# A decoder block on one core: operand tiles and row loads at the start of the feed-forward stage

## The chip, the core and the metric

The kernel runs on one core of one Trainium2 chip. A core has TensorE (PE; matmuls, with the load of the stationary operand shown as PEld), VectorE (DVE), ScalarE (ACT), GpSimd (POOL), SyncE (SP) and 16 DMA engines. All loads and stores of this kernel are issued from SP, in one queue, in a fixed order. The metric is the device time of one execution in microseconds. Three runs of the kernel before gave 2730.93 (median), 2728.78 and 2732.68 us.

## What is computed

One decoder layer for one sequence of 2048 tokens, model width 1024, all in float32. The first half is the token mixer (windowed attention beside an mLSTM, merged and projected); the second half, where the change lies, is a gated feed-forward stage of width 2816:

```python
mix = merged @ w_out[l]
x = x + gate_m[:, None, :] * rms_norm(mix, g_post_mix[l])
h2 = modulate(rms_norm(x, g_pre_ffn[l]), shift_f, scale_f)
ff = (jax.nn.silu(h2 @ w_ffn_gate[l]) * (h2 @ w_ffn_up[l])) @ w_ffn_down[l]
x = x + gate_f[:, None, :] * rms_norm(ff, g_post_ffn[l])
```

## The kernel before

**Precision.** A float32 product is made of three fast ones: each operand is split into a high part (a cast on ACT, line 1353) and a low part (source minus high part, on DVE, line 1354), and `mm` (line 204) issues high x high, high x low and low x high. A tile of 128 x 512 is a unit (256 KB), a tile of 128 x 2048 a big buffer (1 MB).

**Products of sums.** Each block product of 2 x 2 blocks is done with seven products instead of eight. `PROD` lists them as pairs of a weight block or weight sum (11, 12, S2, 22, S1, S3, S4) and an operand (11, 21, T2, T4, T1, T3, 22). The operands 11, 21, 22 are quarters of h2; T1 to T4 are sums of quarters. Every operand has a high and a low tile of four units each, seven pairs in all, kept in `HC` while the gate and up products run. T3 is read by the sixth product, 22 by the seventh.

**Building the operands.** `h_combine(b2, ...)` does that for one half (1024 tokens) of the sequence: for each of four steps k it loads the normalised rows `x1n`, transposes them on PE, scales and shifts them on ACT, forms the sums on DVE and splits them. For the first half it runs inside the last output projection of the mixer. There SBUF is short: three tiles (T2 high, T2 low, T4 high) lie in a pool `hcp` which takes the place of the closed mixer pool `kvp` (line 1362), and the others in big buffers, of which there are 14 (`big`). Two operands are parked: 22 goes to `hc_d` in DRAM (line 1416), and so does T3, of which only the high part is made (line 1418). `rest_of_hc` brings them back in the first gate/up pair: eight loads into units (line 1431), for 22 four casts (line 1433), and eight subtractions (line 1434).

**Gate and up.** `gate_up(b2)` runs 11 pairs p. A pair is seven gate parts, then seven up parts, of 12 matmuls each. Their results go through `combine` (P1 copied on ACT in line 1497, U2 in line 1503, U4 in line 1508) into 16 units in the pool `fpool`, which takes the place of the mixer's `mpool` and `tpool` (names `tm` and `tx`) once these are closed. For the first half each pair also loads two rows of down weights into a big buffer (line 1530), forms their sums and stores four (line 1539); sums of the previous pair's results are stored in line 1581, and results in line 1569.

**Late rows.** The last block's rows of x1 are normalised late: the pairs p = 1 to 4 of the first half end with `norm_rows(3, t)`, which loads a row tile in two halves (line 1548), squares them on ACT with a running sum (line 1549), forms the reciprocal root (POOL, line 475), scales on ACT (line 560) and stores to `x1n` (line 561), which the second half's `h_combine` reads.

**What sets the order.** The program is written as a stream of parts and steps; `run2` loads and prepares weights some parts ahead (four in gate and up). What is written is then ordered for each engine by a planner that plays the program against modelled durations and, whenever an engine is free, takes the earliest written instruction that is ready by its model. That order is fixed before the run; on the chip each engine waits for real. `tc.keep_in_program_order` pins an instruction behind everything written earlier on its engine. Buffers of one kind (units, big buffers) are handed out in written order as they come free.

Of the kernel before, what the change touches and what calls it, by code (L numbers as in the profile page):

```python
# [10 lines left out]
F32 = mybir.dt.float32  # L11
F32R = mybir.dt.float32r
I32 = mybir.dt.int32
U32 = mybir.dt.uint32
AF = mybir.ActivationFunctionType
ALU = mybir.AluOpType
# [3 lines left out]
P = 128  # L20
# [3 lines left out]
TB = 512  # L24
NT = TB // P
NBLK = S // TB
# [45 lines left out]
def decoder_block(ctx: ExitStack, tc: tile.TileContext, a: dict, out: bass.AP, dbg=None):  # L72
    nc = tc.nc
    V, A, G, T = nc.vector, nc.scalar, nc.gpsimd, nc.tensor
# [18 lines left out]
    def nm(s):  # L93
        uid[0] += 1
        return f"{s}{uid[0]}"
# [10 lines left out]
    def tm(shape, dtype=F32):  # L106
        return mpool.tile(shape, dtype, tag="tm", name=nm("tm"), bufs=9)

    def big(shape, dtype=F32):
        t = bpool.tile([P, 2048], dtype, tag="big", name=nm("big"))  # L110
        return t.rearrange("p (k c) -> p k c", k=shape[0])
# [64 lines left out]
    for i in range(HD // 2):  # L176
        f = np.float32(10000.0) ** np.float32(np.float32(-2.0) * np.float32(i) / np.float32(HD))
# [300 lines left out]
    HC, HR = {}, {}  # L478

    def hc_part(name, i):  # L480
        st = HC.setdefault(name, [None, None])
        if st[i] is None:
            st[i] = big([4, TB], F32R)
        return st[i]
# [135 lines left out]
    x1 = [tc.dram_tile([TB, D], F32, name=f"x1_{b}") for b in range(NBLK)]  # L620
# [719 lines left out]
    def unit():  # L1340
        if "pool" not in F:
            return tm([P, TB])
        return F["pool"].tile([P, TB], F32, tag="w", name=nm("w"), bufs=16)

    def quad(t):
        return t.rearrange("p (k c) -> p k c", k=4)

    def split_unit(src, hi=None, lo=None):
        if hi is None:
            t = split_tile("hl")  # L1350
            hi, lo = t[:, :TB], t[:, TB:]
        v = (lambda t: quad(t)) if len(src.shape) == 3 else (lambda t: t)
        A.copy(v(hi), src)  # L1353
        V.tensor_tensor(v(lo), src, v(hi).bitcast(F32), op=ALU.subtract)  # L1354
        return hi, lo
# [3 lines left out]
    def open_hc():  # L1359

        p1k.close()
        hcp = ctx.enter_context(tc.tile_pool(name="hcp", bufs=1, side="right", reuse_waits="tile"))
        HC.clear()
        t2h, t2l, t4h = [hcp.tile([P, 4, TB], F32R, name=f"hc{x}") for x in ("T2h", "T2l", "T4h")]
        hcp.tile([P, 8], F32, name="hc_end")
        HC["T2"] = [t2h, t2l]
        HC["T4"] = [t4h, None]

    def four(t):
        return [t[:, i * 4:(i + 1) * 4, :] for i in range(4)]  # L1370
# [4 lines left out]
    def h_combine(b2, rows, quarters, sums):  # L1375


        wait = b2 == 0
        QUADS = ((0, 0), (0, 1), (1, 0), (1, 1))

        def load(k):
            xk = rows()
            for j, (half, i) in enumerate(QUADS):
                c0 = (k + 4 * half) * P
                nc.sync.dma_start(xk[j], x1n[b2 * 2 + i][:, c0:c0 + P].rearrange("(t p) c -> p t c", p=P))
            return xk

        xn = load(0)
        yield 9000.0 if wait else 13000.0
        for k in range(4):  # L1390
            xk = xn
            v = {}
            for j, (half, i) in enumerate(QUADS):
                kk = k + 4 * half
                ps = mix_tile()
                for t in range(4):
                    transpose(ps[:, t * P:(t + 1) * P], xk[j][:, t, :])
                q = quarters()
                A.activation(q, ps, AF.Identity, scale=s2[:, kk:kk + 1], bias=sh2[:, kk:kk + 1])
                v[f"{half + 1}{i + 1}"] = q  # L1400
                if i:
                    yield 1500.0
            if k < 3:
                xn = load(k + 1)
            v["T1"] = sums()
            V.tensor_tensor(v["T1"], v["12"], v["11"], op=ALU.subtract)
            v["T2"] = sums()
            V.tensor_tensor(v["T2"], v["22"], v["T1"], op=ALU.subtract)
            V.tensor_tensor(v["12"], v["22"], v["12"], op=ALU.subtract)
            v["T3"] = v.pop("12")  # L1410
            for name in NAMES:
                if name == "T4":
                    v["T4"] = sums()
                    V.tensor_tensor(v["T4"], v["21"], v["T2"], op=ALU.subtract)
                if wait and name in ("T3", "22"):
                    nc.sync.dma_start(hc_d[:, ("T3", "22").index(name), k, :], v[name])
                    if name == "T3":
                        A.copy(hc_part("T3", 0)[:, k, :], v[name])
                else:
                    split_unit(v[name], hc_part(name, 0)[:, k, :], hc_part(name, 1)[:, k, :])  # L1420
                    if not wait:
                        yield 1500.0
            yield 10000.0 if wait else 1000.0

    hc_d = tc.dram_tile([P, 2, 4, TB], F32, name="hc_d")

    def rest_of_hc(i):
        name = ("T3", "22")[i]
        for k in range(4):
            u = unit()  # L1430
            nc.sync.dma_start(u, hc_d[:, i, k, :])
            if name == "22":
                tc.keep_in_program_order(A.copy(hc_part("22", 0)[:, k, :], u))
            tc.keep_in_program_order(V.tensor_tensor(hc_part(name, 1)[:, k, :], u, HC[name][0][:, k, :].bitcast(F32), op=ALU.subtract))  # L1434

    def a_operands(raw, spare):

# [101 lines left out]
                nc.sync.dma_start(ws_d[:, i, p, :], q[n])  # L1539
        return load, sums  # L1540

    def norm_rows(blk, t):
        sx = small.tile([P, 2], F32, tag="sx", name=nm("sx"), bufs=4)
        xy = []
        for h2 in range(2):
            c = slice(h2 * TB, (h2 + 1) * TB)
            xr, y0 = unit(), unit()
            nc.sync.dma_start(xr, x1[blk][t * P:(t + 1) * P, c])
            tc.keep_in_program_order(A.activation(y0, xr, AF.Square, accum_out=sx[:, h2:h2 + 1]))
            xy.append((xr, y0, c))  # L1550
        norm_out(xy, t, x1n[blk], sx)

    def gate_up(b2):
        late = None
        for p in range(NP):
            g = {}

            def done_g(qd, t, in_psum, g=g):
                g[qd] = unit()
                A.activation(g[qd], t, AF.Sigmoid)  # L1560
                V.tensor_tensor(g[qd], t, g[qd], op=ALU.mult)

            def done_u(qd, t, in_psum, p=p, g=g):
                V.tensor_tensor(g[qd], t, g[qd], op=ALU.mult)

                names = {"11": "11", "12": "21", "21": "12", "22": "22"}
                F["a", names[qd]] = g[qd]
                if qd != "12":
                    nc.sync.dma_start(as_d[b2][:, IDX[names[qd]], p, :], g[qd])
                    return  # L1570
                g["all"] = {n: F.pop(("a", n)) for n in ("11", "12", "21", "22")}

            def a_sums(p=p, g=g):
                a_ = g["all"]
                s1_, s2_, s4_ = unit(), unit(), unit()
                V.tensor_tensor(s1_, a_["21"], a_["22"], op=ALU.add)
                V.tensor_tensor(a_["21"], a_["11"], a_["21"], op=ALU.subtract)
                V.tensor_tensor(s2_, s1_, a_["11"], op=ALU.subtract)
                V.tensor_tensor(s4_, a_["12"], s2_, op=ALU.subtract)
                for n, t_ in (("S1", s1_), ("S3", a_["21"]), ("S2", s2_), ("S4", s4_)):  # L1580
                    nc.sync.dma_start(as_d[b2][:, IDX[n], p, :], t_)

            gp, up = (list(pair_parts(w, p * 256, done, unit, unit, mix_tile)) for w, done in ((wg, done_g), (wu, done_u)))
            load, sums = down_weights(p)
            if F.get("late") is not None and p == 0:
                def a_step():
                    if F["late"]:
                        F["late"].pop(0)()

                for part in gp + up:  # L1590
                    part.after = a_step
            yield from gp[:2]
            if b2 + p == 0:
                yield lambda: rest_of_hc(0)
            if late:
                yield late
            yield from gp[2:4]
            if b2 + p == 0:
                yield lambda: rest_of_hc(1)
            if b2 == 0:  # L1600
                yield load
            yield from gp[4:] + up[:3]
            if b2 == 0:
                yield sums
            yield from up[3:]
            late = a_sums
            if b2 == 0 and 1 <= p <= NT:
                yield lambda t=p - 1: norm_rows(NBLK - 1, t)
        yield late

    IDX = {x: i for i, (x, _) in enumerate(PROD)}
# [248 lines left out]
```

## Time and profile before

| | |
|---|---|
| runs shown | 2730.93 us median, 2728.78 to 2732.68 |
| profiled execution | 2731.52 us, of which the span from first to last instruction is 2729.8 us |
| granted TensorE clock, mean | 0.994 |
| last matmul of the mixer's output projection | 1417.90 us |
| gate and up, first half | from 1418.13 us |

A row of waits names the engine, tile and line that waited, then what it waited for, then the us in total, the number of times and the longest; the name of a line such as L204 is that of the helper which issued the instruction. In the order of time a row gives start, length, engine, line, operation, out<-in by the program's names, the count of merged instructions, and in brackets the idle time before and what ended it. A row of windows gives for a stretch its length, the busy time of PE, PEld, DVE, ACT and POOL (with counts), the granted PE clock, the DMA engines' busy share and GB/s.

### The profile page before, as it was taken

To read this page: it belongs to the slowest core of one execution; us is meant where nothing else is said; L and a number is where in the kernel's file an instruction comes from. 1 tells how busy PE (TensorE), PEld (TensorE's weight loads), DVE (VectorE), ACT (ScalarE), POOL (GpSimd) and SP (SyncE) were. 2 spreads that over 40 slices of the span, in tenths; PEclk is the share of its full clock that TensorE was granted. 3 is DMA by queue.
4 is the path that set the end of the run, shared out by engine and by line. 5 is a ranking of instruction groups with operands and counts; after the bars stand their busy time and mean duration, and the time that the engine had idled before them with its cause. 6 is when DMAs were issued, how large, how long until landed. Compare 5 with 4: busy or idle time off the path is not lost.

```text
span 2729.8 us, 35753 instructions
## 1 busy us (share of the span) xinstructions
PE 2641.6 (97%) x12310; PEld 2133.7 (78%) x12310; DVE 1999.4 (73%) x3954; ACT 1287.9 (47%) x2510; POOL 153.2 (6%) x189
## 2 busy tenths in 40 slices
PE   6998999999999899999999999999999999999998
PEld 4766688888877668888877878888777888888886
DVE  7959878767786978876677677776677666766456
ACT  5555644445755654344563443335554333333444
POOL 2010002100101000110000000000000000000000
PEclk8999999999999999999999999999999999999999
DMA  7754445687675545577765555446675332324566
GB/s 248 243 172 159 139 143 178 217 329 254 218 247 163 174 151 170 182 237 281 249 212 200 182 182 164 147 144 212 201 266 195 110 108 93 108 97 147 181 213 216
DMA packets 355222, 513.99 MB, mean 188 GB/s; under 512 B 25296, under 2 KB 213836, under 8 KB 349920
## 3 DMA queue, kind: packets, MB, share of 16 engines
q1 hardware_dynamic: 355040, 511.71, 56.5%
q8 instruction: 97, 1.59, 0.2%
q14 instruction: 85, 0.70, 0.1%
HBM read 358.17 MB, written 145.06 MB: 184 GB/s over the span
## 4 chain that ended last, share of the span: by engine, by line
PE 75%; DVE 8%; DMA 4%; issue 4%; ACT 2%; POOL 0%; SPq 0%; DVEq 0%; POOLq 0%; ACTq 0%
PE acc L204 53%; PE mix L204 21%; DVE hl L1354 2%; PE mix L209 1%; DMA w<-x 1%; ACT hl L1353 1%; DMA raw<-as_d 1%; DMA at_d<-tx 1%; DVE tx L1132 1%; DMA raw<-in_w_ffn_down_dram 0%; DMA tx<-in_w_ada_dram 0%; DVE tx L578 0%; DVE big L1354 0%; DMA w<-hc_d 0%; POOL rs L475 0%
## 5 line engine op out<-in xcount | busy, mean ns | idle before, releaser
L204 PE MATMUL acc<-big,hl 128*128 128x512 f32 x3936 | 946.6, 394 | 13.1 <-ACT tx L805 6.8
L204 PEld LDWEIGHTS acc<-big,hl 128*128 128x128 f32 x3936 | 733.8, 189 | 181.2 <-issue 10.1
L1353 ACT CAST hl<-raw 128x512 fp32r<-128x512 f32 x732 | 439.9, 621 | 488.8 <-PE acc L204 227.7
L1354 DVE TENSOR_TENSOR hl<-raw,hl 128x512 fp32r<-128x512 f32 x732 | 497.7, 696 | 193.0 <-ACT hl L1353 192.3
L204 PE MATMUL acc<-whi,big 128*128 128x512 f32 (+1 forms) x1280 | 378.8, 376 | 18.8 <-ACT big L518 8.4
L204 PE MATMUL mix<-big,hl 128*128 128x512 f32 x1232 | 333.9, 393 | 6.8 <-DVE big L1434 6.0
L204 PEld LDWEIGHTS acc<-whi,big 128*128 128x128 f32 x1280 | 234.3, 190 | 65.4 <-ACT big L518 8.5
L204 PEld LDWEIGHTS mix<-big,hl 128*128 128x128 f32 x1232 | 231.8, 188 | 58.5 <-DVE big L1434 6.4
L204 PE MATMUL acc<-wlo,big 128*128 128x512 f32 (+1 forms) x640 | 240.1, 378 | 4.1 <-DVE wlo L260 4.1
L204 PE MATMUL acc<-hl,hl 128*128 128x512 f32 x1008 | 237.1, 393 | 5.4 <-DVE hl L1354 3.5
L204 PEld LDWEIGHTS acc<-hl,hl 128*128 128x128 f32 x1008 | 186.9, 188 | 50.7 <-DVE hl L1354 9.1
L204 PE MATMUL mix<-hl,hl 128*128 128x512 f32 x792 | 183.0, 391 | 2.0 <-ACT hl L1353 1.0
L204 PEld LDWEIGHTS mix<-hl,hl 128*128 128x128 f32 x792 | 147.8, 188 | 36.3 <-DVE hl L1354 3.4
L260 DVE TENSOR_TENSOR wlo<-raw,whi 128x1024 fp32r<-128x1024 f32 (+1 forms) x96 | 109.3, 1138 | 73.0 <-ACT whi L259 66.6
L204 PE MATMUL acc<-big,whi 128*128 128x512 f32 x512 | 154.9, 391 | 0.0
L259 ACT CAST whi<-raw 128x1024 fp32r<-128x1024 f32 (+1 forms) x96 | 94.4, 984 | 126.2 <-PE acc L204 124.2
L204 PEld LDWEIGHTS acc<-wlo,big 128*128 128x128 f32 x640 | 121.9, 191 | 30.1 <-DVE wlo L260 5.6
L475 POOL TENSOR_TENSOR rs<-ms,nhalf 128x1 f32<-128x1 f32 (+1 forms) x56 | 43.1, 781 | 1652.0 <-DVE ms L473 1519.3
L204 PE MATMUL acc<-hcT2h,hl 128*128 128x512 f32 x352 | 118.4, 397 | 4.4 <-ACT w L1497 4.4
L204 PE MATMUL mix<-hcT4h,hl 128*128 128x512 f32 x352 | 117.4, 395 | 0.0
L204 PEld LDWEIGHTS acc<-big,whi 128*128 128x128 f32 x512 | 95.7, 188 | 19.5
L204 PE MATMUL acc<-big,wlo 128*128 128x512 f32 x256 | 96.4, 393 | 0.0
(332 smaller groups left out, 3392.7 us busy)
## 6 DMA issues: line engine op xcount, KB each, us to landing
raw<-in_w_in_dram SPq DMA_DIRECT2D x48, 1024.0 KB
as_d<-w SPq DMA_DIRECT2D x154, 256.0 KB
raw<-as_d SPq DMA_DIRECT2D x70, 512.0 KB
raw<-in_w_ffn_gate_dram SPq DMA_DIRECT2D x22, 1024.0 KB
raw<-in_w_ffn_up_dram SPq DMA_DIRECT2D x22, 1024.0 KB
raw<-ws_d SPq DMA_DIRECT2D x40, 512.0 KB
tx<-in_w_ada_dram SPq DMA_DIRECT2D x64, 256.0 KB
y_d<-tm SPq DMA_DIRECT2D x64, 256.0 KB
```

The lines of the kernel that those rows point to most:

```text
L204: T.matmul(o, lhsT=lhsT, rhs=rhs, start=start, stop=stop, skip_group_check=resumed)
L209: T.transpose(o, i, ident[:k, :k])
L259: A.copy(hv, src)
L260: V.tensor_tensor(lv, src, hv.bitcast(F32), op=ALU.subtract)
L475: G.tensor_tensor(r[:, :n], ms[:, :n], nhalf[:, :n], op=ALU.pow)
L1132: V.scalar_tensor_tensor(ac, u[:, j:j + TB], col("conv_w", j * 8 + f), ac, op0=ALU.mult, op1=ALU.add)
L1353: A.copy(v(hi), src)
L1354: V.tensor_tensor(v(lo), src, v(hi).bitcast(F32), op=ALU.subtract)
```

## The change

T4's low part gets a tile of its own in `hcp`. T3 is split fully inside `h_combine` (a subtraction instead of a store). Only 22 is parked; `load_22` brings it back by one load of 1 MB into the place of its own low part, and `split_22` casts and subtracts from there, both in the first pair, no longer pinned to the written order. `norm_rows` is divided: `load_late` issues the two loads between the gate parts and the up parts, `norm_late` does the rest at the end of the pair, its Squares no longer pinned.

```diff
-        t2h, t2l, t4h = [hcp.tile([P, 4, TB], F32R, name=f"hc{x}") for x in ("T2h", "T2l", "T4h")]
+        t2h, t2l, t4h, t4l = [hcp.tile([P, 4, TB], F32R, name=f"hc{x}") for x in ("T2h", "T2l", "T4h", "T4l")]
         hcp.tile([P, 8], F32, name="hc_end")
         HC["T2"] = [t2h, t2l]
-        HC["T4"] = [t4h, None]
+        HC["T4"] = [t4h, t4l]
...
-                if wait and name in ("T3", "22"):
-                    nc.sync.dma_start(hc_d[:, ("T3", "22").index(name), k, :], v[name])
-                    if name == "T3":
-                        A.copy(hc_part("T3", 0)[:, k, :], v[name])
+                if wait and name == "22":
+                    nc.sync.dma_start(hc_d[:, k, :], v[name])
                 else:
                     split_unit(v[name], hc_part(name, 0)[:, k, :], hc_part(name, 1)[:, k, :])
...
-    hc_d = tc.dram_tile([P, 2, 4, TB], F32, name="hc_d")
-
-    def rest_of_hc(i):
-        name = ("T3", "22")[i]
+    hc_d = tc.dram_tile([P, 4, TB], F32, name="hc_d")
+
+    def load_22():
+        nc.sync.dma_start(hc_part("22", 1).bitcast(F32), hc_d)
+
+    def split_22():
+        hi, lo = (hc_part("22", i) for i in range(2))
         for k in range(4):
-            u = unit()
-            nc.sync.dma_start(u, hc_d[:, i, k, :])
-            if name == "22":
-                tc.keep_in_program_order(A.copy(hc_part("22", 0)[:, k, :], u))
-            tc.keep_in_program_order(V.tensor_tensor(hc_part(name, 1)[:, k, :], u, HC[name][0][:, k, :].bitcast(F32), op=ALU.subtract))
+            split_unit(lo[:, k, :].bitcast(F32), hi[:, k, :], lo[:, k, :])
...
-    def norm_rows(blk, t):
+    rows = {}
+
+    def load_late(blk, t):
+        rows[t] = []
+        for h2 in range(2):
+            c = slice(h2 * TB, (h2 + 1) * TB)
+            rows[t].append((unit(), c))
+            nc.sync.dma_start(rows[t][-1][0], x1[blk][t * P:(t + 1) * P, c])
+
+    def norm_late(blk, t):
         sx = small.tile([P, 2], F32, tag="sx", name=nm("sx"), bufs=4)
         xy = []
-        for h2 in range(2):
-            c = slice(h2 * TB, (h2 + 1) * TB)
-            xr, y0 = unit(), unit()
-            nc.sync.dma_start(xr, x1[blk][t * P:(t + 1) * P, c])
-            tc.keep_in_program_order(A.activation(y0, xr, AF.Square, accum_out=sx[:, h2:h2 + 1]))
+        for h2, (xr, c) in enumerate(rows.pop(t)):
+            y0 = unit()
+            A.activation(y0, xr, AF.Square, accum_out=sx[:, h2:h2 + 1])
             xy.append((xr, y0, c))
         norm_out(xy, t, x1n[blk], sx)
...
             yield from gp[:2]
             if b2 + p == 0:
-                yield lambda: rest_of_hc(0)
+                yield load_22
             if late:
                 yield late
             yield from gp[2:4]
             if b2 + p == 0:
-                yield lambda: rest_of_hc(1)
+                yield split_22
             if b2 == 0:
                 yield load
-            yield from gp[4:] + up[:3]
+            yield from gp[4:]
+            if b2 == 0 and 1 <= p <= NT:
+                yield lambda t=p - 1: load_late(NBLK - 1, t)
+            yield from up[:3]
             if b2 == 0:
                 yield sums
             yield from up[3:]
             late = a_sums
             if b2 == 0 and 1 <= p <= NT:
-                yield lambda t=p - 1: norm_rows(NBLK - 1, t)
+                yield lambda t=p - 1: norm_late(NBLK - 1, t)
```

## Prediction

> **What bounds the kernel now.** I read the page's engine totals first, then what TensorE (PE) waited for from the first feed-forward matmul on, then a table of windows, then the order of time around the longest wait.
>
> ```profile
> span 2729.8 us, 35753 instructions
> ...
> PE 2641.6 (97%) x12310; PEld 2133.7 (78%) x12310; DVE 1999.4 (73%) x3954; ACT 1287.9 (47%) x2510; POOL 153.2 (6%) x189
> ```
>
> PE is busy 2641.6 of 2729.8 us. The change takes no matmul away, so it can only touch PE's waits and PE's pace. The waits of PE from 1418 us to the end, costliest first (us in total, times, longest):
>
> ```profile
> PE mix L204 <- DVE big L1434: 6.0, 1, 6.0
> PE acc L204 <- ACT w L1497: 4.4, 4, 1.3
> PE acc L204 <- DVE hl L1354: 3.5, 5, 1.2
> ```
>
> The first is one wait for line 1434, the low parts made in `rest_of_hc`. In order of time on PE, the queue of SP, DVE and ACT:
>
> ```profile
> 1430.39 0.40 PE L204 MATMUL acc<-hcT2h,hl 128*128 128x512 f32 x1
> 1436.75 2.93 PE L204 MATMUL mix<-big,hl 128*128 128x512 f32 x6 [5.96 <-DVE big L1434]
> 1439.48 4.54 PE L204 MATMUL acc<-big,hl 128*128 128x512 f32 x14
> ...
> 1452.69 0.39 PE L204 MATMUL mix<-hcT4h,hl 128*128 128x512 f32 x1
> ```
>
> ```profile
> 1428.33 0.38 SPq L1520 DMA_DIRECT2D raw<-in_w_ffn_gate_dram  x1
> 1429.05 0.42 SPq L1818 DMA_DIRECT2D gg_f<-gg_f_d  x1
> 1429.53 5.99 SPq L1431 DMA_DIRECT2D w<-hc_d  x8
> 1436.04 1.61 SPq L1530 DMA_DIRECT2D big<-in_w_ffn_down_dram  x3
> ```
>
> ```profile
> 1436.00 1.35 DVE L1434 TENSOR_TENSOR big<-w,big 128x512 fp32r<-128x512 f32 x2 [5.67 <-DMA w<-hc_d]
> 1438.59 2.56 ACT L1433 CAST big<-w 128x512 fp32r<-128x512 f32 x4 [6.66 <-DMA w<-hc_d]
> 1441.60 2.49 DVE L1434 TENSOR_TENSOR big<-w,big 128x512 fp32r<-128x512 f32 x4
> ```
>
> SP issues the eight `hc_d` loads only from 1429.53, the first lands at 1436.0, and until then PE, DVE (5.67) and ACT (6.66) all stand. So the stall is the load of T3, not arithmetic. It leaves a second loss, in the windows (us, then PE, PEld, DVE, ACT, POOL busy, granted clock, DMA share, GB/s):
>
> ```profile
> 1350.00:1389.00 39.00, 39.00 (x193) 32.39 (x192) 37.85 (x57) 28.06 (x43) 0.00 (x0) 1.00 0.69 225
> 1430.00:1440.00 10.00, 4.04 (x12) 2.88 (x11) 4.33 (x8) 2.46 (x5) 0.00 (x0) 0.76 1.03 376
> 1430.80:1452.69 21.89, 15.94 (x59) 12.96 (x60) 14.08 (x23) 8.68 (x15) 0.00 (x0) 0.84 0.78 302
> 1452.69:1471.91 19.22, 19.22 (x85) 15.78 (x84) 13.53 (x23) 5.44 (x10) 0.00 (x0) 1.00 0.61 192
> ```
>
> 1452.69 and 1471.91 are successive starts of the part that reads T4: seven parts of 12, 84 matmuls, in 19.22 us, or 0.2288 us each. From 1436.75 to 1452.69 five parts, 60 matmuls, take 15.94 us; at full pace 60 x 0.2288 = 13.73. So 2.21 us go to the clock that the stall leaves behind (0.84 granted in that window). [...]
>
> The second wait is line 1497, the copy of P1 on ACT. Between 1500 and 1650 us, PE's waits, ACT's waits for the rows, then the order of time on SP, ACT and PE:
>
> ```profile
> PE acc L204 <- ACT w L1497: 3.4, 3, 1.3
> ```
>
> ```profile
> ACT w L1549 <- DMA w<-x: 25.7, 6, 6.6
> ```
>
> ```profile
> 1500.83 0.42 SPq L1548 DMA_DIRECT2D w<-x  x1
> 1506.20 0.38 SPq L1530 DMA_DIRECT2D big<-in_w_ffn_down_dram  x1
> ...
> 1507.14 0.42 SPq L1548 DMA_DIRECT2D w<-x  x1
> ```
>
> ```profile
> 1502.41 0.59 ACT L1508 COPY w<-acc 128x512 f32<-128x512 f32 x1 [2.10 <-PE acc L204]
> ...
> 1513.20 0.63 ACT L1549 ACTIVATE w<-w 128x512 f32<-128x512 f32 x1 [5.73 <-DMA w<-x]
> ...
> 1513.83 0.57 ACT L1497 COPY w<-acc 128x512 f32<-128x512 f32 x1
> ```
>
> ```profile
> 1514.45 0.50 PE L204 MATMUL acc<-hcT2h,hl 128*128 128x512 f32 x1 [1.12 <-ACT w L1497]
> ...
> 1592.72 0.50 PE L204 MATMUL acc<-hcT2h,hl 128*128 128x512 f32 x1 [0.96 <-ACT w L1497]
> ...
> 1632.75 0.50 PE L204 MATMUL acc<-hcT2h,hl 128*128 128x512 f32 x1 [1.31 <-ACT w L1497]
> ```
>
> The second half row is issued at 1507.14, behind a down-weight load that held SP; the Square (L1549) waits 5.73 us for it at the head of ACT, P1's copy stands behind the Square, and PE behind the copy. Three of the four late pairs show it: 1.12 + 0.96 + 1.31 = 3.39 us.
>
> **The change, part by part.**
>
> *T3 complete in the mixer, T4's low part in its own tile.* Removed: four stores and four loads of T3, and the wait of 5.96. Five parts follow it, all with other operands in SBUF except the last product (22). Gain 5.96 + 2.21 = 8.17 us. The number of big buffers held in `h_combine(0)` stays eight (T4's low part leaves, T3's comes), so none has to wait there. The new tile takes the place of the closed mixer pool; the last reads of its values are long past when T4's low part is first written (after 1359 us):
>
> ```profile
> L204 PE MATMUL mix<-vmt,tm x32: 271/275/277, 1206.4 to 1238.8; 128*128 128x129 f32 x32
> ```
>
> *Four subtractions move into the mixer's tail.* They are the same instruction as L1434: four in 2.49 us, a pitch of 0.60. DVE is busy 37.85 of 39.00 us between 1350 and 1389 (window row above), so there they aren't free. The tightest place:
>
> ```profile
> 1373.37 0.61 ACT L1418 CAST big<-tm 128x512 fp32r<-128x512 f32 x1
> ...
> 1376.09 1.22 DVE L260 TENSOR_TENSOR wlo<-raw,whi 128x1024 fp32r<-128x1024 f32 x1
> ...
> 1377.55 0.39 PE L204 MATMUL acc<-wlo,big 128*128 128x512 f32 x1
> ```
>
> The low weights are ready at 1376.09 + 1.22 = 1377.31 and read at 1377.55: 0.24 us of slack. The casts of T3's first two quarters (L1418, the second at 1373.37) lie ahead, and both new subtractions are written before this L260, so I take them to run ahead of it: 2 x 0.60 - 0.24 = 0.96 us of new PE wait. The later L260s then have this shift as slack. Bounds: 0, if the planner puts them behind, and 1.6 (three ahead, 1.80 - 0.24). I take 0.96.
>
> *22 by one load, split in place.* The four casts and four subtractions stay; only when they run changes. One 1 MB load needs one free big buffer and no units. Buffers of the mixer's last matmul become free with it:
>
> ```profile
> 1417.90 0.39 PE L204 MATMUL acc<-whi,big 128*128 128x512 f32 x1
> ```
>
> SP can then issue from about 1418.3, ahead of gate weights and gg. How long 1 MB takes:
>
> ```profile
> 1398.60 0.39 SPq L1520 DMA_DIRECT2D raw<-in_w_ffn_gate_dram  x1
> ...
> 1404.90 0.69 DVE L1448 TENSOR_TENSOR tm<-raw 128x512 f32<-128x512 f32 x1 [2.95 <-DMA raw<-in_w_ffn_gate_dram]
> ```
>
> 6.3 us, so 22 is there at 1424.6 and split well before PE wants it: T3 and T1 alone take 2 x 12 x 0.2288 = 5.5 us from 1430.8, to 1436.3. Cost 0. The other bound: SP keeps it at 1429.53. 2.5 MB (gate, gg, 22) are then queued; before, 1.75 MB were in at 1436.0 and 2.75 MB at 1438.59, so about 1437.9, plus 0.62 cast and 0.69 subtraction: 1439.2, a wait of 2.9 us. I take 0, since a buffer is free eleven microseconds earlier; 2.9 goes to the range.
>
> *Late rows half a pair ahead.* Two loads move before three up parts, some 19 us earlier by program order; the Squares lose their pin. Past them on SP now lie the up weights and the four down-sum stores; behind the Squares on ACT lie casts and copies. If the rows have landed, the 3.39 us go. The bounds are 3.39 and 0; I take 3.39, since a row's load needed 6.1 us (issued 1507.14, Square at 1513.20) against half a pair. No unit is short: two more are held through the up half, when P1, U2, U4, four gates and one sum leave eight of the sixteen.
>
> *A fourth buffer for down weights* (ten operands held instead of eleven) lets L1530 wait less. SP alone waits there, so 0; if those loads run ahead of the last x1 stores, 2 MB at 376 GB/s hold the unit buffers under them up to 5.6 us.
>
> **Sum:** -5.96 - 2.21 - 3.39 + 0.96 = -10.60 us. The profiled span 2729.8 would become 2719.2; from the median 2730.93 that is **2720.3 us**.
>
> **The rivals.**
>
> *22 takes over the stall.* For it: SP showed this order before, gg ahead of `hc_d`, and the split is no longer pinned, so ACT may stand before it as it did for 6.66 us. Against it: the freed buffer. A wait of 2.9 us and its share of clock, 2.21 x 2.9/5.96 = 1.1: -10.6 + 4.0 = -6.6, **2724.3**. [...]
>
> *The rows are still late,* because SP puts them behind the down-sum stores (before, the first one went out right behind them at 1500.83): -10.6 + 3.39 = -7.2, **2723.7**.
>
> *The wait changes its place within the first pair.* The down-weight loads go ahead of the x1 stores, units come 5.6 us later, U2's copy and with it the T1 part wait; PE has only the T3 part (2.75) as cover: +2.9 and 1.1 for clock, and with late rows too: about -3.2, **2727.7**, which is no change that one can tell.
>
> *Slower: unpinned Squares block ACT in mid-pair.* Planned for data that is thought to be there, a Square stands at the head of ACT with U4's copy and the casts behind it. Price: the four pairs waited 25.7 us, 6.4 a pair; the cover on ACT at that place is 2.10 us (L1508 row), so 4.3 a pair, 17.3 in all: -10.6 + 17.3 = +6.7, **2737.6**. It decides from 10.6/4 = 2.65 us a pair on. [...] Against it: the loads are earlier by half a pair, and PE's casts are four parts ahead.
>
> **How the numbers follow.** Main case 0.50; 22 takes over 0.13; rows late 0.12; place changed 0.10; ACT blocked 0.15. A measurement of this kernel can tell about 0.2%, 5.5 us: faster means below 2725.5. The first three cases lie there, less 0.07 for their spread into no change (0.05) and beyond it (0.02): faster 0.68, within 0.15, slower 0.17. Range: low end 2716 (no cost in the tail 0.96, and up to 3.3 of the 3.5 us of L1354 waits, if the fourth buffer or the new order removes them), high end 2733 (the place changed, and half of the blocked cases); some 0.07 lie below and 0.10 above. Its own range for the main case is 2717 to 2723.
>
> **What would show it.** Right: no PE wait for the split of T3 or 22 in the first pair, granted clock 1.00 there, `hc_d` loaded by one issue near 1418, no ACT wait for w<-x above 1 us, and a PE wait of about 1 us for `wlo` near 1377. Wrong: a PE wait near 1436 on the split of 22, ACT standing before Squares or casts of 22, or the load of 22 still behind gg.

## The result, and the profile after

The changed kernel takes **2723.59 us** (median of 7 runs, 2721.44 to 2727.14) against 2731.41 us for the kernel before in runs beside it (7 runs, 2728.55 to 2737.71). The ratio is 0.997 with a 95% interval of 0.996 to 0.9979: faster by 5.7 to 10.9 us. The forecast was 2720.3 us, faster. The profiled execution of after took 2727.14 us, the slowest of its seven; its span is 4.4 us below that of before.

From the page of after, the span and the engines' totals:

```profile
span 2725.4 us, 35775 instructions
...
PE 2644.5 (97%) x12310; PEld 2136.0 (78%) x12310; DVE 1999.1 (73%) x3954; ACT 1287.0 (47%) x2510; POOL 152.6 (6%) x189
```

The matmuls are as many as before. PE's waits of after from 1418 us to the end:

```profile
PE mix L204 <- ACT hl L1353: 3.1, 5, 0.8
PE acc L204 <- DVE hl L1354: 2.9, 4, 1.2
PE acc L204 <- ACT hl L1353: 2.5, 4, 0.7
...
PE acc L204 <- ACT w L1500: 0.7, 1, 0.7
```

The 6.0 us for T3's low parts and the 4.4 us for P1's copy are gone. New at the head of the list stand waits for `hl`, the cast weights. The time can be placed with four windows, first of before, then of after (us, then busy time and instructions of PE, PEld, DVE, ACT, POOL, granted clock, DMA share, GB/s):

```profile
60.00:240.00 180.00, 160.56 (x863) 123.30 (x862) 140.36 (x356) 96.62 (x235) 12.23 (x14) 0.99 0.64 207
1357.00:1425.00 68.00, 68.00 (x325) 56.47 (x324) 56.66 (x91) 41.49 (x71) 2.62 (x3) 1.00 0.57 194
1427.00:1475.00 48.00, 41.31 (x169) 33.40 (x170) 33.30 (x55) 18.23 (x31) 0.00 (x0) 0.93 0.67 236
1500.00:1650.00 150.00, 146.60 (x639) 119.31 (x638) 105.83 (x180) 59.88 (x116) 2.16 (x4) 1.00 0.55 181
```

```profile
60.00:240.00 180.00, 161.28 (x830) 124.15 (x830) 135.07 (x344) 95.08 (x231) 12.12 (x13) 0.94 0.62 202
1357.00:1425.00 68.00, 68.00 (x326) 56.53 (x325) 59.31 (x94) 45.80 (x79) 0.54 (x1) 1.00 0.62 199
1427.00:1475.00 48.00, 45.17 (x191) 34.84 (x190) 34.08 (x57) 16.65 (x29) 1.74 (x2) 1.00 0.71 241
1500.00:1650.00 150.00, 150.00 (x657) 122.91 (x657) 111.75 (x188) 62.84 (x118) 2.17 (x4) 1.00 0.56 181
```

Read the matmul counts of PE. In the first pair (1427 to 1475 us) after starts 22 more in the same 48 us, 22 x 0.2288 = 5.0 us; in the late pairs (1500 to 1650) 18 more, 4.1 us. In the mixer's tail (1357 to 1425) PE has no gap in either. And in a stretch that the change doesn't touch (60 to 240) after starts 33 fewer, at a granted clock of 0.94 instead of 0.99: this profile of after is 5.5 us behind before's when its 1000th matmul starts. From there to its last matmul it gains 10.1 us.

The same can be put as a ledger, which the experiments use too. Every execution has 12310 matmuls; from the start of one to that of another, less 0.2288 us for each matmul between them, is what PE lost to waits and to the clock. Matmul 6700 is one of the mixer's last, 7000 lies behind the first pair's stall, 7750 behind the late pairs:

| lost, us | 6700 to 7000 | 7000 to 7750 |
|---|---|---|
| before | 9.97 | 4.34 |
| after | 4.73 | 0.00 |

So the first pair gave 5.2 us where 8.17 were forecast, and the late rows 4.3 where 3.39 were. What is left in the first pair, in order of time on PE:

```profile
1431.68 3.01 PE L204 MATMUL mix<-big,hl 128*128 128x512 f32 x12
1435.40 3.29 PE L204 MATMUL acc<-big,hl 128*128 128x512 f32 x12 [0.71 <-ACT hl L1353]
1439.40 3.29 PE L204 MATMUL mix<-big,hl 128*128 128x512 f32 x12 [0.71 <-ACT hl L1353]
...
1446.17 3.01 PE L204 MATMUL acc<-big,hl 128*128 128x512 f32 x12 [0.68 <-ACT w L1500]
...
1449.92 0.50 PE L204 MATMUL mix<-hcT4h,hl 128*128 128x512 f32 x1 [0.74 <-ACT hl L1353]
```

Four waits, 2.84 us. The parts at 1435.40 and 1439.40 belong to the up matrix: PE runs two of them ahead of the gate's T2 part. On ACT of after one sees why:

```profile
1438.73 0.62 ACT L1353 CAST hl<-raw 128x512 fp32r<-128x512 f32 x1 [3.38 <-PE acc L204]
1439.25 0.58 ACT L1494 COPY w<-acc 128x512 f32<-128x512 f32 x1
```

P1's copy comes at 1439.25; before it came at 1427.09, or 1432.4 with the lag of 5.3 us that after has here. It is 6.9 us late, and the T2 part adds its product to the same PSUM tile that this copy reads, so it has to wait for the copy. Three of the four weight buffers hold parts that wait for P1, so T3's and the two up parts pass through the fourth, one after another: each cast must wait until the part before it has been read. P1 is late by what SP's queue did. Here it is before, then after, with SP's longest wait at a down-weight load in after:

```profile
1410.04 1.00 SPq L615 DMA_DIRECT2D tm<-in_x_dram  x2
1419.37 5.56 SPq L579 DMA_DIRECT2D x<-tx  x6
1427.07 0.98 SPq L579 DMA_DIRECT2D x<-tm  x2
```

```profile
1412.33 0.33 SPq L1426 DMA_DIRECT2D big<-hc_d  x1
1414.67 0.38 SPq L1517 DMA_DIRECT2D raw<-in_w_ffn_up_dram  x1
1423.41 0.38 SPq L1527 DMA_DIRECT2D big<-in_w_ffn_down_dram  x1
1423.84 0.93 SPq L615 DMA_DIRECT2D tm<-in_x_dram  x2
1424.87 0.59 SPq L1527 DMA_DIRECT2D big<-in_w_ffn_down_dram  x1
1426.21 0.99 SPq L579 DMA_DIRECT2D x<-tx  x2
1428.14 0.38 SPq L1527 DMA_DIRECT2D big<-in_w_ffn_down_dram  x1
1428.87 2.91 SPq L579 DMA_DIRECT2D x<-tx  x4
1433.59 0.32 SPq L579 DMA_DIRECT2D x<-tm  x1
1434.12 0.38 SPq L1527 DMA_DIRECT2D big<-in_w_ffn_down_dram  x1
1434.81 0.32 SPq L579 DMA_DIRECT2D x<-tm  x1
```

```profile
SPq L1527 <- PE acc L204: 8.5, 1, 8.5
```

A down-weight load stands ahead of the last residual rows (L615) and waits 8.5 us for its big buffer, until the mixer's last matmuls are done; before, those rows went out at 1410.04, and all down weights went behind the last x1 stores (x<-tm, 1427.07). The stores then pay a second time. By the semaphores in the traces, the six x<-tx stores of before landed 2.0 to 2.1 us after their issue; after, with down weights ahead of them in the queue, they took 7.9 to 9.6 us. P1's copy goes into the place of the first of these tiles, and so has to wait for its store: it landed at 1421.4 before and at 1434.1 after, 7.4 us later when the lag of 5.3 us is taken off. The copy itself shows no wait in after: from 1434.1 to 1439.25 it stands behind casts in ACT's fixed order, the last of which waited 3.38 us for PE. That the planner chose this order because its model had the buffers late is argued, not shown.

### The profile page after: what moved, and what is told of

It reads as the page before. It is cut to its first block, busy times and chain, and to the rows that moved or that the text cites. A ratio compares the mean times of both kernels' runs of the same rounds, so it can differ in the third digit from the quotient of the medians.

```text
span 2725.4 us, 35775 instructions
## 1 busy us (share of the span) xinstructions
PE 2644.5 (97%) x12310; PEld 2136.0 (78%) x12310; DVE 1999.1 (73%) x3954; ACT 1287.0 (47%) x2510; POOL 152.6 (6%) x189
## 4 chain that ended last, share of the span: by engine, by line
PE 77%; DVE 7%; issue 4%; DMA 2%; ACT 2%; POOL 0%; SPq 0%; DVEq 0%; POOLq 0%; ACTq 0%
PE acc L204 54%; PE mix L204 22%; DVE hl L1354 1%; PE mix L209 1%; ACT hl L1353 1%; DMA at_d<-tx 1%; DMA raw<-as_d 1%; DVE tx L1132 1%; DMA raw<-in_w_ffn_down_dram 1%; DMA raw<-ws_d 0%; DVE w L1664 0%; DVE big L1354 0%; DVE big L552 0%; POOL rs L475 0%; DMA x1n<-tm 0%
## 5 line engine op out<-in xcount | busy, mean ns | idle before, releaser
L204 PE MATMUL mix<-big,hl 128*128 128x512 f32 x1056 | 263.9, 390 | 1.6 <-ACT hl L1353 1.0
L204 PEld LDWEIGHTS mix<-big,hl 128*128 128x128 f32 x1056 | 197.7, 188 | 46.0 <-DVE hl L1354 1.8
```

The lines of the kernel that those rows point to most:

```text
L204: T.matmul(o, lhsT=lhsT, rhs=rhs, start=start, stop=stop, skip_group_check=resumed)
```

## The experiments

The runs were made in three groups of four, in the order of the table. Each time stands beside the kernel before on the same chip (its medians there 2732.84, 2731.89 and 2730.23 us). The last two columns are the ledger of each kernel's one profile, in us.

| kernel | us | ratio, 95% interval | lost 6700-7000 | lost 7000-7750 |
|---|---|---|---|---|
| the change again | 2722.4 | 0.9964, 0.995 to 0.9978 | 4.62 | 0.00 |
| first operands only | 2725.78 | 0.9978, 0.9969 to 0.9987 | 4.67 | 3.37 |
| late rows only | 2728.39 | 0.9986, 0.9978 to 0.9995 | 9.90 | 0.09 |
| down loads in order | 2719.19 | 0.9953, 0.9937 to 0.9969 | 1.53 | 0.00 |
| rows early, Squares pinned | 2727.44 | 0.9986, 0.9977 to 0.9995 | 9.66 | 0.08 |
| rows late, Squares free | 2732.78 | 1.0003, 0.9994 to 1.0012 | 8.86 | 1.95 |
| T3 and 22 parked, one load each | 2726.79 | 0.998, 0.9972 to 0.9989 | 9.28 | 0.00 |
| down loads in order, split later | 2717.17 | 0.9945, 0.9932 to 0.9959 | 1.05 | 0.00 |
| both parked, down loads in order | 2721.96 | 0.9965, 0.9952 to 0.9977 | 2.95 | 0.00 |
| eight more subtractions | 2723.48 | 0.9974, 0.9963 to 0.9985 | 4.63 | 0.00 |
| down loads in order, again | 2719.41 | 0.9959, 0.9946 to 0.9971 | 1.36 | 0.00 |
| the same and split later, again | 2718.8 | 0.9959, 0.9946 to 0.9973 | 1.05 | 0.00 |

**The change again**, unedited.

> The changed kernel again, unedited. In its profile after, the product matmuls ran 5.4 us behind before's already at 237 us, in code that both kernels share. Theory A: this is half-clock time that falls now here, now there from one execution to the next; the time stays near 2723.6, and in this profile the lag at 237 us is another one (between -4 and +5.4). Theory B: the change itself has moved something early; then the lag at 237 us is 5.4 again, and the gain behind it is 10 us.

2722.4 us, and the 1000th matmul lies 1.6 us behind before's instead of 5.5. Theory A holds. Other profiles show the same: the first one of the kernel with the later split is 5.1 us behind at that matmul, its second 0.6. The half-clock time that the theory speaks of stands in the trace of after from 214 to 218 us, for one: a granted clock of 0.50, where before has 1.00. A window of the first profile with the later split shows a granted clock of 0.94:

```profile
130.00:240.00 110.00, 96.90 (x468) 69.80 (x467) 75.44 (x199) 54.00 (x154) 9.02 (x9) 0.94 0.59 186
```

**The two halves apart.** First the operands alone: after, with the late rows put back.

```
-            if b2 == 0 and 1 <= p <= NT:
-                yield lambda t=p - 1: load_late(NBLK - 1, t)
...
-                yield lambda t=p - 1: norm_late(NBLK - 1, t)
+                yield lambda t=p - 1: norm_rows(NBLK - 1, t)
```

> The first-operand half of the change alone (fourth tile, 22 alone parked, one load); late rows loaded and squared as before. By the recorded sum -5.96 - 2.21 + 0.96 = -7.2 us against before. By the profile after, where the first pair gained 5.2 us: about -5, with P1's copy late by some 7 us and short PE waits for ACT's casts near 1435 to 1450 us. The three PE waits on P1's copy between 1500 and 1650 us (3.39 in sum) stand.

Then the rows alone: before, with `load_late` and `norm_late` in place of `norm_rows`.

> The late rows alone (loaded half a pair ahead, Squares unpinned); T3 and 22 parked and loaded as before. By the recorded term -3.39 us against before; by the comparison of the two traces between pairs two and five, -4.35. The rival that unpinned Squares block ACT gives +13.9 (17.3 - 3.39). The stall of 5.96 us near 1431 stays. If the two halves add, this and the first-operand half alone sum to the whole change, -7.8 us by the medians.

By the medians -7.1 and -4.5 us, together -11.5 beside the -10.4 of the whole change in the same group: they add within the intervals. The ledger is sharper: each half takes its own column and leaves the other. The first half stops at 4.67 us lost, so the new waits are its own. The rival that unpinned Squares block ACT is refuted (late rows only is faster, not 13.9 us slower).

**What makes P1 late.** After, with the down-weight loads of the first pair held in program order, behind the x1 stores.

```
-            nc.sync.dma_start(st["raw"], wdn[p * 256:(p + 1) * 256, :].rearrange("(k p) c -> p k c", p=P))
+            d = nc.sync.dma_start(st["raw"], wdn[p * 256:(p + 1) * 256, :].rearrange("(k p) c -> p k c", p=P))
+            if p == 0:
+                tc.keep_in_program_order(d)
```

> The changed kernel with the first pair's down-weight loads held in program order, so that on SP's queue no down-weight load stands ahead of the last mixer rows and x1 stores. Theory C: the head of SP made the last x1 rows late, P1's copy with them, and PE paid 2.84 us of waits for casts and about 1.4 of slower starts; then this kernel is 3 to 4 us below the changed one, P1's copy lies near 1427 to 1432 instead of 1439 and no PE wait on a cast is left near 1435 to 1450. Theory D: P1 is late because the units come free with the mixer's end, whatever stands on SP; then no change within 1 us.

2719.19 us, 3.2 below the changed kernel in the same group. SP's queue of this kernel, then its ACT and its window:

```profile
1410.90 1.05 SPq L615 DMA_DIRECT2D tm<-in_x_dram  x2
1422.07 5.57 SPq L579 DMA_DIRECT2D x<-tx  x6
1429.17 0.98 SPq L579 DMA_DIRECT2D x<-tm  x2
...
1430.91 2.63 SPq L1527 DMA_DIRECT2D big<-in_w_ffn_down_dram  x4
```

```profile
1431.14 0.58 ACT L1494 COPY w<-acc 128x512 f32<-128x512 f32 x1
```

```profile
1427.00:1475.00 48.00, 47.29 (x204) 37.83 (x203) 38.13 (x62) 18.55 (x31) 0.83 (x1) 1.00 0.75 270
```

The rows go out at 1410.90 again. P1's copy comes 8.1 us earlier than in after, 3.9 us when the lags of the two profiles at that place (5.3 and 1.1 us) are taken off, and PE starts 204 matmuls where after started 191: 13 x 0.2288 = 3.0 us. One wait of 0.71 us for a cast is left. The six x<-tx stores land 2.0 to 2.1 us after their issue again, by the semaphores. Theory C holds in size and place. The edit moves all the down loads at once, so which of them does the harm, and how much is owed to the fourth buffer, stays open.

**Which half of the rows' edit.** On the kernel before: loads early with the Squares still pinned, and Squares unpinned with the loads where they were.

```
-            A.activation(y0, xr, AF.Square, accum_out=sx[:, h2:h2 + 1])
+            tc.keep_in_program_order(A.activation(y0, xr, AF.Square, accum_out=sx[:, h2:h2 + 1]))
```

> Before's kernel with the late rows loaded half a pair ahead, the Squares pinned to their place as before. Theory (the load's place makes the gain): the rows have landed, no PE wait on P1's copy is left between 1500 and 1650 us, and the time is that of the rows alone, -4.4 us against before by the traces. Rival (the pin holds ACT): the waits stay, 0 +- 1.

```
-            tc.keep_in_program_order(A.activation(y0, xr, AF.Square, accum_out=sx[:, h2:h2 + 1]))
+            A.activation(y0, xr, AF.Square, accum_out=sx[:, h2:h2 + 1])
```

> Before's kernel with the Squares unpinned and the row loads at the end of the pair as before. Theory (the load's place makes the gain): ACT still waits some 6 us for a half row in each late pair, PE still waits for P1's copy, 0 +- 1 us against before (a cast that now stands behind the first Square could add up to 2 us a pair). Rival (the pin held ACT): the 3.4 to 4.4 us go without any load being moved.

The place of the load makes the gain: with the Squares pinned the column is as empty as after (0.08). In after one sees the distance, SP and then ACT:

```profile
1478.47 1.39 SPq L1546 DMA_DIRECT2D w<-x  x2
```

```profile
1502.99 0.63 ACT L1553 ACTIVATE w<-w 128x512 f32<-128x512 f32 x1
...
1503.61 0.62 ACT L1553 ACTIVATE w<-w 128x512 f32<-128x512 f32 x1
```

The loads go out 24.5 us ahead of the Squares, which start without a wait. Unpinning alone leaves ACT waiting:

```profile
1509.78 0.63 ACT L1549 ACTIVATE w<-w 128x512 f32<-128x512 f32 x1 [4.63 <-DMA w<-x]
```

Its time is that of before within the interval, while its ledger shows 2.4 us less lost in the late pairs than before. PE's waits for P1's copy between 1500 and 1650 us sum to 1.1 us there, beside 3.4 before. Whether the pin is worth something by itself is not settled by this one profile.

**Must T3 be complete in the mixer?** After, with T3 parked again beside 22, each back by one load into its own low tile.

```
-                if wait and name == "22":
-                    nc.sync.dma_start(hc_d[:, k, :], v[name])
+                if wait and name in ("T3", "22"):
+                    nc.sync.dma_start(hc_d[:, ("T3", "22").index(name), k, :], v[name])
...
-        nc.sync.dma_start(hc_part("22", 1).bitcast(F32), hc_d)
+        for i, n in enumerate(("T3", "22")):
+            nc.sync.dma_start(hc_part(n, 1).bitcast(F32), hc_d[:, i])
```

`split_22` loops over both in the same way.

> The changed kernel with T3 parked again beside 22: both come back by one 1 MB load each into their own low tile, ahead of the gate weights on SP; T3's casts and subtractions move back out of the mixer. It tells whether the stall of 5.96 us went because T3 is complete in the mixer, or because the load no longer waits behind gg and for unit buffers. Theory E (queue and units): both loads go out near 1408 to 1412 us, T3 is split by 1420, PE wants it at 1428: no stall, the changed kernel's time within 1.5 us. Theory F (T3 must be complete): a PE wait on T3's split of 2 us or more near 1428, and the time 3 to 8 us above the changed kernel.

Both theories miss a half. PE never waits for T3 (E), but the time is 4.4 us above the changed kernel's of the first group and the first pair loses 9.28 us, nearly as much as before: the price that theory F named, without the wait that it named. SP, ACT and PE of this kernel:

```profile
1431.11 0.38 SPq L1529 DMA_DIRECT2D big<-in_w_ffn_down_dram  x1
1431.86 0.42 SPq L579 DMA_DIRECT2D x<-tm  x1
```

```profile
1440.60 0.59 ACT L1496 COPY w<-acc 128x512 f32<-128x512 f32 x1 [5.36 <-DMA x<-tm]
```

```profile
1441.24 0.50 PE L204 MATMUL acc<-hcT2h,hl 128*128 128x512 f32 x1 [2.65 <-ACT w L1496]
```

P1's copy waits for the last x1 store itself, which was issued at 1431.86 behind down-weight loads and holds its buffer until 1440.6. So the down loads went into this kernel as well:

> T3 and 22 both parked and brought back by one load each (as in two_parked), with the first pair's down-weight loads held in program order. In two_parked PE waited no more for T3, but 2.65 us for P1's copy, whose buffer was held until the last x1 store had landed, behind down-weight loads in the queue. Theory J (what stands ahead of the x1 stores sets P1, and T3's place doesn't matter): the loss over the first pair falls from two_parked's 9.3 us to below 3 us, and the time lies within 2 us of pin_down's. Theory F again (T3 must be complete in the mixer, since its casts and subtractions are late work on ACT and DVE): the first pair still loses 5 us or more.

The loss falls from 9.28 to 2.95 us and the time to 2721.96 us. Theory J holds for the loss, just; the time lies 2.55 us above the same order with T3 complete, where within 2 was expected. So T3 from the mixer is worth some 1.6 us by the ledger (2.95 against 1.36), and the rest of the stall of before was a matter of where T3's loads stood in SP's queue and which buffers they waited for; these two runs don't separate one from the other.

**22's split later.** The kernel with the down loads in order, and `split_22` yielded behind `gp[4:6]`.

> The changed kernel with the down-weight loads of the first pair held in program order (as in pin_down) and 22's split written two parts later, so that its four casts and subtractions don't stand ahead of the mixer's last evacuations on ACT and DVE. Theory G: the split ahead of them made x1's last rows and P1's copy about 1 us late in pin_down, and PE paid 0.71 us of a wait for a cast and about 0.5 of a slower start: 1 us below pin_down, P1's copy near 1430 or before. Rival H: the casts of 22 now stand ahead of an up cast near 1428 and PE waits there: 1 to 2 us above pin_down.

> pin_down again, beside late_split on one chip. By the losses over the first pair (1.5 us against late_split's 1.1) late_split is 0.4 us ahead; by the medians of the runs so far 2.0.

> late_split again, beside pin_down on one chip: 0.4 to 2 us below it, and 4 to 6 us below the changed kernel. In its profile the lag at 237 us is another than the 5.1 us of its first (between -1 and 6), since that is half-clock time that differs from one execution to the next.

Measured in different groups the later split reads 2.0 us lower; side by side it is 2718.8 against 2719.41, which the runs don't tell apart. The ledger has 0.3 us for it (1.05 against 1.36): neither G nor H is shown. The lag at the 1000th matmul is 0.6 us in its second profile, as expected another than in its first. Either version beats the kernel before: by the second measurements the one takes 0.9946 to 0.9971 of its time, the other 0.9946 to 0.9973. Against the changed kernel the one comparison in a group (3.2 us) and the ledger (4.62 - 1.53 = 3.1 us) agree, while the intervals of the two ratios to before overlap.

**Room in the mixer's tail.** After, with T3's four low subtractions made three times each.

```
+                    for _ in range(2 if wait and name == "T3" else 0):
+                        V.tensor_tensor(lo, v[name], hi.bitcast(F32), op=ALU.subtract)
```

> The changed kernel with each of T3's four low subtractions made three times, so eight more subtractions of 0.60 us in the mixer's tail, 4.8 us of DVE. The recorded term was +0.96 us for four, by a slack of 0.24 us at one low weight; the profile after shows no such wait. Theory K (the order puts low weights ahead of operand subtractions, so the tail has room): no PE wait on L260 above 0.5 us, the time within 1 us of the changed kernel. Theory L (the tail is full: DVE shows no gap from 1357 to 1405 us after the change): PE waits 2 to 4.8 us between 1370 and 1425 us, and the time rises as much.

PE's waits of this kernel between 1357 and 1425 us, and the window:

```profile
PE acc L204 <- DVE big L597: 0.8, 1, 0.8
PE acc L204 <- DVE wlo L260: 0.5, 1, 0.5
```

```profile
1357.00:1425.00 68.00, 66.70 (x316) 54.89 (x315) 63.21 (x102) 43.89 (x76) 1.42 (x2) 1.00 0.57 187
```

Of 4.8 us put in, 1.3 come out as PE waits, and 1.7 are lost from matmul 6600 to 6700, where after loses none: between K and L. The median, 2723.48 us, can't tell so little. After shows no wait in that window, and DVE is busy 47.59 of the 48 us from 1357 to 1405 there: the tail took four more subtractions free in the changed kernel's profiles. The margin is thin. The second profile of the kernel with the down loads in order, which has the same four, shows one wait of 0.4 us for `wlo`, and loses 0.5 us between matmuls 6600 and 6700.

## Why the prediction was right, and where its sizes were not

The direction and the mechanism held. By its terms:

- **T3's stall, -5.96, and the clock behind it, -2.21: right.** Both are gone; the granted clock is 1.00 from 1427 to 1475 where it was 0.93. With the down loads in order the first pair gives 9.97 - 1.53 = 8.4 us, beside the 8.17 of the sum.
- **The down-weight loads (the term for a fourth buffer), 0: the step that failed.** The sum said that SP alone waits at those loads, and kept up to 5.6 us as the bound if they run ahead of the last x1 stores. They do. SP waits 8.5 us at the first, which holds up the last residual rows, and the stores behind them take some 6 us longer to land (7.9 instead of 2.0 for the first), close to the 5.6 of the bound. On TensorE it costs 4.62 - 1.53 = 3.1 us, shown by holding the loads in order; that the freed buffer let them forward is not shown. This is the rival "the wait changes its place within the first pair" in a milder form: its cause was right, but the late units reach PE mostly through the one weight buffer left for the casts (three of four waits), and the granted clock stays at 1.00. It was given 0.10; the truth was a sum of the main case and of it.
- **Late rows, -3.39: right, and too small.** They gave 4.34 - 0.00 = 4.3 us. The term summed idle times, and a wait costs more than its idle time: (4.34 - 3.39) / 3 = 0.32 us each, beside an estimate of 0.27 from the rows: the matmul behind a wait takes 0.50 instead of 0.39 us, and 0.39 - 0.2288 us of the one ahead of it is no longer overlapped.
- **Four subtractions in the tail, +0.96: wrong.** No wait for `wlo` shows. The prediction took both subtractions to run ahead of the low weights of one matmul, because they are written ahead; the order came out anew, and nobody waited. Its lower bound, 0, is what happened in the changed kernel; the wait that it named came with eight more (0.5 us), and once without (0.4 us, in the second profile with the down loads in order).
- **22's load and split, 0: right,** and earlier than said: issued at 1412.33, not 1418.3, when a matmul of the projection released its big buffer, some 11 us ahead of the mixer's last (1423.22).
- **Unpinned Squares: refuted** by the late rows alone. **Rows still late** and **22 takes over the stall: refuted** by the rows at 1478.47 and by the waits of after, which have none on 22.

The sum of what was measured is -5.2 - 4.3 = -9.6 us in the profile, beside -10.6 forecast and -7.8 and -10.4 by the medians of the two groups. The errors of +3.1 (down loads), -0.96 (tail) and -0.95 (rows) partly cancelled, so that the total came nearer than its terms is partly luck; and the first pair also got rid of a P1 wait of before (0.96 us at 1427.72) that the sum left out. That the profile of after showed only -4.4 is put down to half-clock time in its first 240 us, where its granted clock was 0.92 and before's 0.96 (0.94 and 0.99 from 60 us on).

## What to carry to other kernels

Here a load at the head of SP's queue waited 8.5 us for a buffer and held up the residual rows behind it, and with such loads ahead of them the small stores that followed landed 7.9 to 9.6 us after their issue instead of 2.0 to 2.1. When a change frees a buffer or reorders loads, ask which load will move forward, what stands behind it, and hold it back if that is urgent. Issuing a load early enough that its data have landed removed the whole loss of the late rows (4.34 to 0.08 us), while unpinning what uses it left 1.95. And before crediting a profile's span, compare the two executions in a stretch that the change doesn't touch.

## What the hardware did that I had not expected

The stretches of low granted clock outside the change differ from one execution of the same code to the next: the 1000th matmul of the kernel with the later split lay 5.1 us behind before's in one profile and 0.6 in another, which is as large as the gain in the first pair.

The clock also fell behind a wait much shorter than the 5.96 us of before. In the kernel with both parked, PE stood 2.65 us for P1 (up to 1441.24), and behind it, in windows of 2 us, the granted clock was 0.64 and 0.51:

```profile
1442.00:1444.00 2.00, 2.00 (x7) 1.58 (x6) 0.84 (x2) 1.12 (x2) 0.00 (x0) 0.64 0.33 133
1444.00:1446.00 2.00, 1.64 (x4) 0.73 (x3) 0.46 (x1) 0.32 (x1) 0.00 (x0) 0.51 0.00 0
```

The four waits of after in the first pair, 0.68 to 0.74 us each, left the granted clock at 1.00 (1427 to 1475 us). That the wait of 2.65 us by itself brought the clock down is inferred from this one place: two waits of 0.71 us lie in the 10 us ahead of it.
